# A trunk of one retention and one attention layer: the retention's gates computed 512 columns wide in a place of their own, its transposes and scores moved inside the next unit's projection

## The chip, the cores and the metric

The kernel runs on one core of a Trainium2 chip. A core has five engines that each work through their own list of instructions: TensorE (PE, matrix products; its weight loads are shown as a row of their own, PEld), VectorE (DVE), ScalarE (ACT), GpSimd (POOL) and SyncE (SP, which here only issues the DMA transfers). They meet at semaphores. TensorE writes to PSUM, the accumulator memory of eight banks; the other operands live in SBUF; DRAM is reached by DMA only. The metric is the device time of the whole program in microseconds, the median of three runs.

## The reference, cut to what matters

1024 tokens of width 1024 pass a layer of gated retention and then a layer of gated differential attention. The change touches the retention alone:

```python
proj = h @ w_in_a[layer]                      # h = rmsnorm(x), 1024 x 6144: q, k, v and gate
o = retention(rope(q), rope(k), v)            # 8 heads, q and k 128 wide, v 256 wide, group-normed
y = (o * jax.nn.silu(gate)) @ w_out_a[layer]  # the gate is 2048 wide: 256 columns for each head
x = x + rmsnorm(y, post_norm[layer])
```

The gate of a head depends on the input x alone. It is needed where `o` is multiplied by it, ahead of the output projection.

## The kernel before

**Split products.** All large products are float32 made of three matmuls: both operands are split into a high and a low part (`split`: one ScalarE copy for the high part, one VectorE subtraction for the low part), and `mm3` issues high x high, high x low and low x high for each 128-deep slab (line 100). A product over the model width of 1024 has 8 slabs, so 24 matmuls.

**Units.** The retention runs over 8 heads times 8 chunks of 128 tokens: 64 units, head by head. In a unit, `gemm_qkv` makes q, k and v (512 columns) of one chunk in 24 matmuls. `rotate` applies the rotary tables (two VectorE products, lines 207 and 208, and a GpSimd sum, line 209) and splits v. `gate_and_transpose` makes the 256 gate columns of this head and chunk in another 24 matmuls, then transposes q and k on TensorE (lines 218 and 219), copies them out (line 220) and applies SiLU to the gate (line 221). The unit before this one is finished meanwhile: `score` (line 234, two halves of one fp32 matmul; then lines 235 to 237 for mask and split) sits between slabs 3 and 4 of the next unit's `gemm_qkv`, and `combine` behind that `gemm_qkv`: up to 9 matmuls of 256 columns (tile names `ps<-r,r`), the state's update, the group norm (lines 264 to 268), with the gate multiplied in at line 267, and a store of 128 KB into the DRAM tile `ogd` (line 271).

**What TensorE does in a unit, in order:** 12 matmuls of q/k/v, 2 of the score, 12 of q/k/v, up to 9 of `combine`, 24 of the gate, 2 transposes.

**Weights.** `load_wa` brings a head's weights: eight transfers of 256 KB for q/k/v (12 buffers of tag "w", so four slabs beside the eight in use) and four of 256 KB for the gate (tag "wa", four buffers). Each goes through one of four staging buffers (tag "st") and a `split` (lines 90 and 91). All transfers are issued by SP, in one order.

**What follows.** The output projection goes in two passes over the 8 chunks, heads 0 to 3 and then heads 4 to 7. `prep` loads 512 KB of `ogd` (line 341), transposes it (line 313) and splits it; `gemm0` and `gemm1` make 48 matmuls of 512 columns each; `fin1` transposes the result for the attention layer. Then come the attention's gates (`gate_unit`, tiles `pg<-wbg,x2T`: 24 matmuls of 512 columns for each half of the width and chunk), and its 64 units; neither is touched.

**The order of the instructions** is not the order in the code. A planner in the compiler goes through the instructions by priority (their place in the code), knows each one's cost by a model, and gives every engine a fixed list; a later instruction may go ahead where an earlier one is not ready or has no buffer yet. [...]

Of the kernel before, what the change touches and what calls it, by code (L numbers as in the profile page):

```python
# [18 lines left out]
P = 128  # L19
# [16 lines left out]
def yoco_kernel(ctx: ExitStack, tc: tile.TileContext, a: dict):  # L36
# [11 lines left out]
    gd = dram.tile([S, D], F32, name="gd")  # L48

# [18 lines left out]
    def kt(shape, nm, dt=F32):  # L68
        return sbuf("k", shape, dt, nm)
# [68 lines left out]
    def load_qkv(h, s, tiles):  # L138
        w = wt([P, 2, 512], f"wq{h}{s}")
        tiles.append(w)  # L140
        st = st_([P, 512], "stw")
        nc.sync.dma_start(st, a["wa"][h, s, :, 0:512])
        split(w[:, 0, :], w[:, 1, :], st, g_pre0[:, s : s + 1])

    def load_gate(h, s, tiles):
        if s % 4 == 0:
            w = wta([P, 4, 2, 256], f"wg{h}{s}")
            tiles += [w[:, i] for i in range(4)]
        st = st_([P, 2, 256], "stg")
        nc.sync.dma_start(st, a["wa"][h, s : s + 2, :, 512:768].rearrange("s p c -> p s c"))  # L150
# [3 lines left out]
    def load_wa(h):  # L154
        wq, wg = [], []
        for s in range(NS):
            load_qkv(h, s, wq)
            if s % 2 == 1:
                load_gate(h, s - 1, wg)
        return wq, wg  # L160
# [3 lines left out]
    wq, wg = [], []  # L164
# [16 lines left out]
    w_next = (wq, wg)  # L181
# [10 lines left out]
    def rotate(u):  # L192
        c = u["c"]
        pq, pp, wg = u["pq"], u["pp"], u["wg"]
# [18 lines left out]
    def gate_and_transpose(u):  # L213
        c, qk, qkT = u["c"], u["qk"], u["qkT"]
        pgt = u["pp"][:, 0:256]
        mm3(pgt, [(*xs(c, s), u["wg"][s][:, 0, :], u["wg"][s][:, 1, :]) for s in range(NS)])
        pt = ps("s", 256)
        nc.tensor.transpose(pt[:, 0:P], qk[:, 0:P], ident)
        nc.tensor.transpose(pt[:, P:256], qk[:, P:256], ident)
        nc.scalar.activation(qkT, pt, AF.Copy)  # L220
        nc.scalar.activation(u["og"], pgt, AF.Silu, scale=rstd[:, c : c + 1])
# [19 lines left out]
    def combine(u):  # L241
# [3 lines left out]
        pU, pk = u["pp"][:, 512:768], u["pp"][:, 768:1024]  # L245
# [9 lines left out]
        if c < NC - 1:  # L255
# [15 lines left out]
        nc.sync.dma_start(ogd[c * P : (c + 1) * P, h * DV : (h + 1) * DV], og)  # L271

    prev = None
    early = [ps("g"), ps("g")]
    gemm_qkv(list(enumerate(early)), w_next[0], range(NS))
    for i in range(H * NC):
        h, c = divmod(i, NC)
        if c == 0:
            wq, wg = w_next
        u = {"h": h, "c": c, "wg": wg, "pp": ps("s2", 1024)}  # L280
        u["pq"] = early[i] if i < 2 else ps("g")
        if i >= 2:
            gemm_qkv([(c, u["pq"])], wq, range(0, NS // 2))
        if prev:
            score(prev)
        if i >= 2:
            gemm_qkv([(c, u["pq"])], wq, range(NS // 2, NS))
        rotate(u)
        if prev:
            combine(prev)  # L290
        gate_and_transpose(u)
        prev = u
        if h == 0 and c + 2 < NC:
            if c + 3 < NC:
                load_x(c + 3)
            stats_x(c + 2)
        if c == (1 if h else 5) and h + 1 < H:
            w_next = load_wa(h + 1)
    score(prev)
    combine(prev)  # L300

    def load_wo(src, f, gain, hi, lo):
# [3 lines left out]
        return hi, lo  # L306

# [20 lines left out]
    wo0 = [load_wo(a["woa"], f, None, xw[0][:, f, :], xw[1][:, f, :]) for f in range(4)]  # L328

    def wo_pair():  # L330
        w = wta([P, 2, D], "wo")
        return w[:, 0], w[:, 1]

    wo0 += [load_wo(a["woa"], f, None, *wo_pair()) for f in range(4, 8)]
# [375 lines left out]
def _layout(i):  # L710
# [7 lines left out]
    g = w[:, 4096:6144].reshape(D, H, DV)  # L718
    wa = np.concatenate([qk.reshape(D, H, 256), v, g], axis=2)
    wa = wa.reshape(NS, P, H, 768).transpose(2, 0, 1, 3)  # L720
# [13 lines left out]
        "wa": wa,  # L734
        "woa": np.asarray(i["w_out_a"])[0],
# [25 lines left out]
```

## Time and profile before

| | |
|---|---|
| median of 3 runs (lowest to highest) | 1524.19 us (1524.13 to 1524.55) |
| the profiled execution's own time | 1519.59 us |
| its span, first to last instruction | 1517.8 us |
| PE, PEld busy | 1480.0 us (98%), 1296.0 us (85%) |
| DVE, ACT, POOL busy | 782.9 us (52%), 626.3 us (41%), 266.2 us (18%) |
| DMA moved | 125.63 MB |
| granted TensorE clock over the span | 0.997 |

A row of the groups gives line, engine, operation, output and inputs by the program's names, shape and count, then busy microseconds in all, mean nanoseconds of one, and the idle time of the engine ahead of them. As TensorE overlaps the tail of one matmul with the start of the next, the mean of one is longer than what one costs; the difference of start times in the timeline is the cost. A row of the timeline gives start, duration from the first start to the last end, engine, line, operation and count, and in brackets the idle time ahead of it with what ended it. A row of the stretches gives, for a stretch of time, its length and the busy time and instruction count of PE, PEld, DVE, ACT and POOL, then the granted clock, the share of the DMA engines and the rate.

### The profile page before, as it was taken

What the parts mean: (1) busy time and instruction counts of PE and PEld (TensorE: products, weight loads), DVE (VectorE), ACT (ScalarE), POOL (GpSimd) and SP (SyncE); (2) the same over time, 40 slices, a digit from 0 to 9 for tenths busy, and PEclk for the clock granted to TensorE, in tenths of its full rate; (3) what the DMA queues carried; (4) which work ended last, traced back from release to release, by engine and by line L of the source; (5) the groups of instructions that cost most, each with busy time, mean ns of one, the idle gap of its engine ahead of it and who ended that gap; (6) DMA issues with size and microseconds to landing.
All of it is one profiled execution on the core that took longest, in us unless ns stands there. A gap on an engine that the chain in (4) does not pass through costs nothing.

```text
span 1517.8 us, 23752 instructions
## 1 busy us (share of the span) xinstructions
PE 1480.0 (98%) x8752; PEld 1296.0 (85%) x8752; DVE 782.9 (52%) x1968; ACT 626.3 (41%) x1591; POOL 266.2 (18%) x470
## 2 busy tenths in 40 slices
PE   6999999999999999999999999999999999999998
PEld 5888998888889888888877788988988988987786
DVE  5664645454545443541145511667567577577543
ACT  5542424242424232342244522456455466465421
POOL 1322222212222222200000000222222222222100
PEclk9999999999999999999999999999999999999999
DMA  7430302021211210353244522111011011023352
GB/s 272 146 111 15 97 15 88 22 82 31 60 53 47 62 62 30 98 191 104 98 153 167 190 95 71 34 47 52 10 51 51 11 51 51 12 92 115 116 174 84
DMA packets 70308, 125.63 MB, mean 83 GB/s; under 512 B 7600, under 2 KB 40752, under 8 KB 70192
## 3 DMA queue, kind: packets, MB, share of 16 engines
q1 hardware_dynamic: 70192, 124.11, 25.2%
q8 instruction: 69, 1.13, 0.3%
q14 instruction: 47, 0.39, 0.1%
HBM read 94.72 MB, written 29.36 MB: 82 GB/s over the span
## 4 chain that ended last, share of the span: by engine, by line
PE 80%; DVE 6%; DMA 5%; ACT 4%; issue 4%; POOL 1%; SPq 0%; DVEq 0%; POOLq 0%; ACTq 0%
PE pg L100 54%; PE ps L100 14%; PE ps L526 3%; PE ps L562 3%; PE ps L551 2%; DMA stg<-in_wa 1%; ACT pr L534 1%; DMA stw<-in_wa 1%; PE ps L313 1%; DVE wbh L91 1%; PE ps L234 1%; DMA og<-ogd 1%; PE ps L512 1%; DMA xr<-in_x 1%; DVE m L533 1%
## 5 line engine op out<-in xcount | busy, mean ns | idle before, releaser
L100 PE MATMUL pg<-wq,xT 128*128 128x512 f32 x1536 | 387.6, 402 | 8.8 <-ACT wq L90 7.1
L100 PEld LDWEIGHTS pg<-wq,xT 128*128 128x128 f32 x1536 | 281.5, 190 | 65.0 <-ACT wq L90 7.1
L100 PE MATMUL pg<-wbh,x2T 128*128 128x384 f32 x1536 | 334.6, 353 | 0.0
L100 PEld LDWEIGHTS pg<-wbh,x2T 128*128 128x128 f32 x1536 | 256.4, 189 | 13.0 <-issue 9.3
L106 POOL TENSOR_TENSOR m<-m,mhalf 128x1 f32<-128x1 f32 x152 | 83.3, 548 | 652.8 <-DVE m L105 591.2
L100 PE MATMUL ps<-wg,xT 128*128 128x256 f32 x1536 | 194.8, 283 | 0.0
L100 PEld LDWEIGHTS ps<-wg,xT 128*128 128x128 f32 x1536 | 189.1, 192 | 0.1
L534 ACT ACTIVATE pr<-ps,m 128x256 f32<-128x256 f32 (+7 forms) x128 | 94.0, 737 | 92.1 <-DVE m L533 92.1
L209 POOL TENSOR_TENSOR a<-a 128x256 f32<-128x256 f32 x64 | 48.1, 752 | 340.4 <-DVE a L208 324.9
L533 DVE TENSOR_REDUCE m<-ps 128x1 f32<-128x256 f32 (+7 forms) x128 | 91.1, 753 | 0.0
L100 PE MATMUL pg<-wbg,x2T 128*128 128x512 f32 x384 | 87.9, 390 | 0.8 <-DVE wbg L91 0.8
L90 ACT ACTIVATE r<-pg,tabA 128x256 fp32r<-128x256 f32 x64 | 30.1, 470 | 136.7 <-DVE a L208 136.2
L100 PEld LDWEIGHTS pg<-wbg,x2T 128*128 128x128 f32 x384 | 71.8, 188 | 16.0 <-DVE wbg L91 1.2
L100 PEld LDWEIGHTS ps<-r,r 128*128 128x128 f32 x528 | 72.1, 190 | 8.6 <-ACT r L236 2.6
L235 DVE TENSOR_TENSOR a<-ps,tabA 128x128 f32<-128x128 f32 x64 | 18.5, 289 | 116.5 <-PE ps L234 116.5
L100 PE MATMUL ps<-r,r 128*128 128x256 f32 x528 | 74.8, 283 | 2.4 <-ACT r L236 2.0
L562 PE MATMUL ps<-v,wT 128*128 128x128 f32 x576 | 74.7, 275 | 0.0
L562 PEld LDWEIGHTS ps<-v,wT 128*128 128x128 f32 x576 | 73.2, 191 | 0.7 <-DVE m L105 0.4
L503 POOL TENSOR_TENSOR tabB<-tabB 128x256 f32<-128x256 f32 x64 | 48.5, 758 | 127.9 <-DVE tabB L502 127.6
L207 DVE TENSOR_TENSOR a<-pg,tabA 128x256 f32<-128x256 f32 x64 | 27.0, 423 | 80.6 <-PE pg L100 80.5
L236 ACT ACTIVATE r<-a 128x128 fp32r<-128x128 f32 x64 | 19.8, 309 | 111.6 <-DVE a L235 111.5
L100 PE MATMUL pg<-wo,oh 128*128 128x512 f32 x192 | 59.9, 391 | 0.0
(142 smaller groups left out, 2344.0 us busy)
## 6 DMA issues: line engine op xcount, KB each, us to landing
stw<-in_wa SPq DMA_DIRECT2D x64, 256.0 KB, 3.0
stb<-in_wbh SPq DMA_DIRECT2D x64, 192.0 KB, 2.4
xr<-in_x SPq DMA_DIRECT2D x16, 512.0 KB, 4.2
stg<-in_wa SPq DMA_DIRECT2D x32, 256.0 KB, 3.3
ogd<-a SPq DMA_DIRECT2D x64, 128.0 KB, 1.9
sto<-in_woa SPq DMA_DIRECT2D x16, 512.0 KB, 4.8
og<-ogd SPq DMA_DIRECT2D x16, 512.0 KB, 5.0
y0d<-y SPq DMA_DIRECT2D x8, 512.0 KB, 3.2
```

Of the source, the lines that this page charges most:

```text
L90: nc.scalar.activation(hi, src, AF.Copy, scale=scale)
L100: nc.tensor.matmul(out, l, r, start=(first and i == 0), stop=(last and i == n - 1))
L106: nc.gpsimd.tensor_tensor(out=out, in0=t, in1=mhalf[:, 0:n], op=ALU.pow)
L207: nc.vector.tensor_tensor(out=o4(t1), in0=q4, in1=cb, op=ALU.mult)
L209: nc.gpsimd.tensor_tensor(out=qk, in0=t1, in1=t2, op=ALU.add)
L236: nc.scalar.activation(ss[:, 0, :], sc, AF.Copy)
L503: nc.gpsimd.tensor_tensor(out=r[:, 2], in0=r[:, 0], in1=r[:, 1], op=ALU.add)
L526: nc.tensor.matmul(sc[t][:, c0 : c0 + n], q[rows, ql, qs], k[rows, kl, 0:n], start=(i == 0), stop=(i == 2))
L533: nc.vector.tensor_reduce(out=nm[:, t : t + 1], in_=sc[t][:, :nk], axis=AX.X, op=ALU.max, negate=True)
L534: nc.scalar.activation(pr[t][:, :nk], sc[t][:, :nk], AF.Exp, bias=nm[:, t : t + 1], accum_out=s_[:, t : t + 1])
L551: nc.tensor.transpose(pt[:, k - k0 : k - k0 + P], w[:, k : k + P], ident)
L562: nc.tensor.matmul(po, wT[:, kb * P : (kb + 1) * P], v[:, kb % 4], start=(kb == 0), stop=(kb == b))
```

## The change

The gate leaves the unit. `gate(p, c)` makes the gates of two heads at once, 512 columns in 24 matmuls, applies SiLU (ScalarE, 512 wide) and stores 256 KB into a new DRAM tile `gad`. There are 4 pairs of heads times 8 chunks; pair 0 is made in units 2 to 9, pair p in units 16p to 16p + 7, behind the `combine` that is done in that unit. So 32 units carry a gate (a long unit, 24 more matmuls of 512 columns) and the other 32 none (a short unit). Gate weights of pair 0 are loaded at the start, those of pair p behind units 16p - 5 to 16p - 2, as four transfers of 512 KB. `prep` loads the two 256 KB halves of the gate and multiplies them in on VectorE ahead of its transposes.

The transposes move from the end of their own unit into the next unit's `gemm_qkv`, behind its third slab, and the score moves from behind the fourth to behind the fifth. The first two units are rotated one after the other, and both are transposed and scored inside unit 2. The group norm no longer has the gate in it: the factor `svec` goes into the 128 x 1 column `r`, and one VectorE instruction writes the output from PSUM.

At the start the input statistics of three chunks stand ahead of the gate weights. The square for them is written in place, where a scratch tile was used. The first four of the output projection's weight tiles are loaded ahead of the retention's last units, into the buffers of the gate weights.

```diff
-        junk = kt([P, D], "junk")
-        nc.scalar.activation(junk, xr, AF.Square, accum_out=ssq)
+        nc.scalar.activation(xr, xr, AF.Square, accum_out=ssq)
...
+    def load_gate(p, j):
+        w = wta([P, 2, 2, 512], f"wg{p}{j}")
+        st = st_([P, 2, 512], "stg")
+        nc.sync.dma_start(st, a["wg"][p, 2 * j : 2 * j + 2].rearrange("s p c -> p s c"))
         for i in range(2):
-            split(tiles[s + i][:, 0], tiles[s + i][:, 1], st[:, i], g_pre0[:, s + i : s + i + 1])
+            s = 2 * j + i
+            split(w[:, i, 0], w[:, i, 1], st[:, i], g_pre0[:, s : s + 1])
+            wg[p, s] = w[:, i]
...
     stats_x(0)
-    for s in range(0, NS, 2):
-        load_gate(0, s, wg)
-    nc.sync.dma_start(mask, a["mask"])
     load_x(2)
     stats_x(1)
+    stats_x(2)
+    nc.sync.dma_start(mask, a["mask"])
+    for j in range(4):
+        load_gate(0, j)
+    load_x(3)
...
+    def gate(p, c):
+        pg = ps("s2")
+        mm3(pg, [(*xs(c, s), wg[p, s][:, 0, :], wg[p, s][:, 1, :]) for s in range(NS)])
+        sg = sbuf("v", [P, 512], F32, "sg")
+        nc.scalar.activation(sg, pg, AF.Silu, scale=rstd[:, c : c + 1])
+        nc.sync.dma_start(gad[c * P : (c + 1) * P, p * 512 : (p + 1) * 512], sg)
...
-        pU, pk = u["pp"][:, 512:768], u["pp"][:, 768:1024]
+        pp = ps("s2")
+        pU, pk = pp[:, 0:256], pp[:, 256:512]
...
-        nc.vector.scalar_tensor_tensor(out=og, in0=pU, scalar=mv[:, 0:1], in1=og, op0=ALU.subtract, op1=ALU.mult)
-        nc.vector.tensor_scalar(
-            out=og, in0=og, scalar1=r, scalar2=svec[:, c, h : h + 1], op0=ALU.mult, op1=ALU.mult
-        )
+        nc.vector.tensor_scalar(out=r, in0=r, scalar1=svec[:, c, h : h + 1], scalar2=None, op0=ALU.mult)
+        nc.vector.tensor_scalar(out=og, in0=pU, scalar1=mv[:, 0:1], scalar2=r, op0=ALU.subtract, op1=ALU.mult)
...
+    gates = {(c + 2 if p == 0 else 2 * NC * p + c): (p, c) for p in range(H // 2) for c in range(NC)}
+    late = {2 * NC * p - 5 + j: (p, j) for p in range(1, H // 2) for j in range(4)}
...
+        parts = [f for w in waiting for f in ((transpose_qk, w), (score, w))]
+        at = {2: 0, 4: 1} if len(parts) == 2 else {1: 0, 3: 1, 5: 2, 7: 3}
+        for s in range(NS):
+            gemm_qkv([(c, u["pq"])], wq, [s])
+            if s in at:
+                f, w = parts[at[s]]
+                f(w)
+        for w in waiting[:-1]:
+            combine(w)
+        rotate(u)
+        combine(waiting[-1])
+        waiting = [u]
+        if i in gates:
+            gate(*gates[i])
+        if i in late:
+            load_gate(*late[i])
...
+        if i == H * NC - 4:
+            wo0 = [load_wo(a["woa"], f, None, *wo_pair()) for f in range(4)]
...
         nc.sync.dma_start(og, ogd[t * P : (t + 1) * P, grp * D : (grp + 1) * D])
+        for hf in range(2):
+            g = sbuf("v", [P, 512], F32, "g")
+            cs = slice(hf * 512, hf * 512 + 512)
+            nc.sync.dma_start(g, gad[t * P : (t + 1) * P, grp * D + hf * 512 : grp * D + hf * 512 + 512])
+            nc.vector.tensor_tensor(out=og[:, cs], in0=og[:, cs], in1=g, op=ALU.mult)
```

More of the change, by code (lines that the diff above doesn't have):

```diff
@@ L141, in load_qkv @@
         st = st_([P, 512], "stw")
-        nc.sync.dma_start(st, a["wa"][h, s, :, 0:512])
+        nc.sync.dma_start(st, a["wa"][h, s])
         split(w[:, 0, :], w[:, 1, :], st, g_pre0[:, s : s + 1])
[L145 to L150, printed above, removed]
-        for i in range(2):
-            split(tiles[s + i][:, 0], tiles[s + i][:, 1], st[:, i], g_pre0[:, s + i : s + i + 1])
[L154 to L160, printed above, removed]
+    wg = {}
+    def load_gate(p, j):
+        w = wta([P, 2, 2, 512], f"wg{p}{j}")
+        st = st_([P, 2, 512], "stg")
+        nc.sync.dma_start(st, a["wg"][p, 2 * j : 2 * j + 2].rearrange("s p c -> p s c"))
+        for i in range(2):
+            s = 2 * j + i
+            split(w[:, i, 0], w[:, i, 1], st[:, i], g_pre0[:, s : s + 1])
+            wg[p, s] = w[:, i]
     nc.sync.dma_start(gains, a["gains"])
     load_x(0, parts=2)
-    wq, wg = [], []
+    wq = []
     load_qkv(0, 0, wq)
@@ L211, in rotate, with transpose_qk @@
         split(u["v"][:, 0, :], u["v"][:, 1, :], pq[:, 256:512], avec[:, c, u["h"] : u["h"] + 1])
-    def gate_and_transpose(u):
+    def gate(p, c):
[4 more added lines that the diff above has]
+        nc.sync.dma_start(gad[c * P : (c + 1) * P, p * 512 : (p + 1) * 512], sg)
+    def transpose_qk(u):
         c, qk, qkT = u["c"], u["qk"], u["qkT"]
-        pgt = u["pp"][:, 0:256]
-        mm3(pgt, [(*xs(c, s), u["wg"][s][:, 0, :], u["wg"][s][:, 1, :]) for s in range(NS)])
         pt = ps("s", 256)
+        nc.tensor.transpose(pt[:, P:256], qk[:, P:256], ident)
         nc.tensor.transpose(pt[:, 0:P], qk[:, 0:P], ident)
-        nc.tensor.transpose(pt[:, P:256], qk[:, P:256], ident)
         nc.scalar.activation(qkT, pt, AF.Copy)
-        nc.scalar.activation(u["og"], pgt, AF.Silu, scale=rstd[:, c : c + 1])
         if c < NC - 1:
@@ L306, in load_wo, with wo_pair @@
         return hi, lo
+    def wo_pair():
+        w = wta([P, 2, D], "wo")
+        return w[:, 0], w[:, 1]
+    gates = {(c + 2 if p == 0 else 2 * NC * p + c): (p, c) for p in range(H // 2) for c in range(NC)}
+    late = {2 * NC * p - 5 + j: (p, j) for p in range(1, H // 2) for j in range(4)}
+    early = [ps("g"), ps("g")]
+    gemm_qkv(list(enumerate(early)), wq, range(NS))
+    waiting = []
+    for i in range(2):
+        u = {"h": 0, "c": i, "pq": early[i]}
+        rotate(u)
+        waiting.append(u)
+    for i in range(2, H * NC):
+        h, c = divmod(i, NC)
+        if c == 0:
+            wq, w_next = w_next, []
+        u = {"h": h, "c": c, "pq": ps("g")}
+        parts = [f for w in waiting for f in ((transpose_qk, w), (score, w))]
[7 more added lines that the diff above has]
+            combine(w)
+        rotate(u)
+        combine(waiting[-1])
[4 more added lines that the diff above has]
+            load_gate(*late[i])
+        if h == 0 and c + 1 < NC:
+            if c + 2 < NC:
+                load_x(c + 2)
+            stats_x(c + 1)
+        if c == (1 if h else 5) and h + 1 < H:
+            w_next = []
+            for s in range(NS):
+                load_qkv(h + 1, s, w_next)
+        if i == H * NC - 4:
+            wo0 = [load_wo(a["woa"], f, None, *wo_pair()) for f in range(4)]
+    for f in (transpose_qk, score, combine):
+        f(u)
     def transposed(dst_h, dst_l, src):
@@ L327, in yoco_kernel @@
     xw = [xt([P, 4, D], f"xw{hl}") for hl in range(2)]
[L328 to L334, printed above, removed]
+    wo0 += [load_wo(a["woa"], f, None, xw[0][:, f - 4, :], xw[1][:, f - 4, :]) for f in range(4, 8)]
     wo1 = []
@@ L717, in _layout @@
     v = w[:, 2048:4096].reshape(D, H, DV)
-    g = w[:, 4096:6144].reshape(D, H, DV)
-    wa = np.concatenate([qk.reshape(D, H, 256), v, g], axis=2)
-    wa = wa.reshape(NS, P, H, 768).transpose(2, 0, 1, 3)
+    wa = np.concatenate([qk.reshape(D, H, 256), v], axis=2)
+    wa = wa.reshape(NS, P, H, 512).transpose(2, 0, 1, 3)
+    wg = w[:, 4096:6144].reshape(NS, P, H // 2, 512).transpose(2, 0, 1, 3)
     wi = np.asarray(i["w_in_b"])[0]
```

34 lines of the change are left out of this document (4 added, 30 removed).

## The prediction

> **What bounds the kernel now.** I read the page first, then the groups, then a table of stretches, then the timeline of one quiet unit.
>
> ```profile
> span 1517.8 us, 23752 instructions
> ...
> PE 1480.0 (98%) x8752; PEld 1296.0 (85%) x8752; DVE 782.9 (52%) x1968; ACT 626.3 (41%) x1591; POOL 266.2 (18%) x470
> ...
> L100 PE MATMUL ps<-wg,xT 128*128 128x256 f32 x1536 | 194.8, 283 | 0.0
> ...
> L100 PE MATMUL pg<-wbg,x2T 128*128 128x512 f32 x384 | 87.9, 390 | 0.8 <-DVE wbg L91 0.8
> ```
>
> ```profile
> 30.00:45.00 15.00, 12.48 (x67) 10.54 (x68) 10.71 (x28) 11.23 (x23) 7.40 (x11) 0.89 0.61 217
> ...
> 110.00:650.00 540.00, 539.46 (x3313) 483.70 (x3311) 269.89 (x742) 180.76 (x459) 117.24 (x206) 1.00 0.17 54
> ...
> 177.00:187.00 10.00, 10.00 (x62) 8.91 (x61) 8.07 (x20) 5.12 (x14) 2.52 (x5) 1.00 0.55 172
> ...
> 280.00:289.90 9.90, 9.90 (x62) 8.90 (x61) 4.09 (x12) 2.46 (x7) 2.22 (x4) 1.00 0.05 15
> ```
>
> From 110 to 650 us TensorE is busy for 539.46 of 540 us: there the retention is bound by how many matmuls it issues and how long each holds the engine; only what shortens this list can gain. The other engines matter as soon as they make TensorE wait. DMA is at 0.17 there, so extra traffic is cheap. One quiet unit on TensorE:
>
> ```profile
> 300.89 3.04 PE L100 MATMUL ps<-wg,xT 128*128 128x256 f32 x24
> 303.77 0.27 PE L218 MATMUL ps<-ident,a 128*128 128x128 f32 x1
> ...
> 303.91 2.98 PE L100 MATMUL pg<-wq,xT 128*128 128x512 f32 x12
> 306.73 0.38 PE L234 MATMUL ps<-a 128*128 128x128 f32 x2
> 306.86 3.02 PE L100 MATMUL pg<-wq,xT 128*128 128x512 f32 x12
> 309.72 1.24 PE L100 MATMUL ps<-r,r 128*128 128x256 f32 x9
> 310.79 3.04 PE L100 MATMUL ps<-wg,xT 128*128 128x256 f32 x24
> ```
>
> By starts: the gate takes 303.77 - 300.89 = 2.88 us (120 ns a matmul), the two transposes 0.14, the q/k/v halves 2.82 and 2.86 with 0.13 of score between, `combine` 1.07; 9.90 us in all.
>
> **The change part by part.** The sum is made against the profiled execution (span 1517.8, own time 1519.59 us; the 1.8 us around the span stay) and then taken off the median of 1524.19, which lies 4.6 us above it.
>
> *1. The gate at 512 columns.* Removed: 1536 matmuls of 256 columns, 64 x 2.88 = 184.3 us. Added: 768 of 512 columns. The nearest row is the attention's own gate, `pg<-wbg,x2T`: same shape, 24 in a row, and 87.9 / 384 = 229 ns each, so 24 take 5.49 us and 32 gates 175.8 us: **-8.6 us**. Bounds: the q/k/v halves of the unit above, 2.82 + 2.86 = 5.68 us for 24, would give 32 x 5.68 = 181.8 us, -2.6; the fastest stream of 512 columns in the trace, in the output projection,
>
> ```profile
> 666.24 0.61 PE L100 MATMUL pg<-xw,oh 128*128 128x512 f32 x2
> 666.70 0.39 PE L100 MATMUL pg<-xw,ol 128*128 128x512 f32 x1
> 666.92 0.61 PE L100 MATMUL pg<-xw,oh 128*128 128x512 f32 x2
> ```
>
> has three matmuls in 0.68 us, 5.44 us for 24, and would give -10.2. I take the attention's gate because it has the same operands' layout and length; the q/k/v halves each start behind a break, which the new gate does not.
>
> The Trainium skill (TensorE: Matmul & The Clock Gate, Back-to-back issue gap) gives N / 2.4 + 2.5 ns for a lone warm matmul; by that two narrow ones cost only 2.5 ns more than one wide one, and the estimate from that page would be 768 x 2.5 = 1.9 us instead of 8.6. The rows above disagree: twice 120 against 229 is 11 ns.
>
> *2. Transposes, score and `combine`* stay the same in number. A score inside a 512-column stream costs what it cost; a transpose pair now has wide matmuls on both sides as the score has. Zero, if their inputs are there in time. The start-to-start distances on the other engines:
>
> ```profile
> 280.22 0.42 DVE L207 TENSOR_TENSOR a<-pg,tabA 128x256 f32<-128x256 f32 x1 [1.81 <-PE pg L100]
> ...
> 281.12 0.74 POOL L209 TENSOR_TENSOR a<-a 128x256 f32<-128x256 f32 x1 [5.26 <-DVE a L208]
> ...
> 283.97 0.27 PE L218 MATMUL ps<-ident,a 128*128 128x128 f32 x1
> ...
> 284.47 0.32 SPq L271 DMA_DIRECT2D ogd<-a  x1
> 284.54 0.38 ACT L220 ACTIVATE a<-ps 128x256 f32<-128x256 f32 x1
> ...
> 286.93 0.38 PE L234 MATMUL ps<-a 128*128 128x128 f32 x2
> ...
> 288.01 0.29 DVE L237 TENSOR_TENSOR r<-a,r 128x128 fp32r<-128x128 f32 x1 [0.38 <-ACT r L236]
> ```
>
> A short unit takes TensorE 9.90 - 2.88 = 7.02 us. The rotation needs 281.86 - 280.22 = 1.64 us, plus about 0.2 from the end of q/k/v; in the new order 1.07 (`combine`) + 3/4 of 2.82 = 3.2 us lie between, so 1.3 us are spare. From the transposes to copied q and k is 284.92 - 283.97 = 0.95 us, and that had SiLU in front; the new order gives two slabs, 1.4 us, plus the transposes themselves: 0.5 to 0.7 spare. From the score to the split mask is 288.30 - 286.93 = 1.37 us against three slabs, 2.1: 0.7 spare. In a quiet short unit nothing waits; DVE's 4.09 us and ACT's 2.46 fit into 7.02. The output's store is at 284.47, 4.25 us behind the rotation's start, so its buffer is free before the rotation two units later.
>
> The spare times go where weights are split in a short unit:
>
> ```profile
> 246.21 2.68 ACT L90 ACTIVATE wq<-stw,gains 128x512 fp32r<-128x512 f32 x4
> ...
> 246.95 2.08 DVE L91 SCALAR_TENSOR_TENSOR wq<-stw,gains,wq 128x512 fp32r<-128x512 f32 x3 [1.48 <-ACT wq L90]
> ```
>
> One split of 512 columns holds ACT for 0.67 and DVE for 0.69 us. The next head's slabs come in two groups of four, at the last unit of a head and the first of the next (177 to 187 us above is such a place: DVE 8.07 of 10 us). At each of six boundaries one of these two units is short: 24 splits. The gates of pairs 1 to 3 are 12 transfers of two splits: 24 more, all in short units. In a short unit with four splits DVE has 4.09 + 4 x 0.69 = 6.9 of 7.02 us: full, while it was 7 to 8 of 9.9 before. Queued behind a split on DVE or ACT stand lines 207, 220 and 235 to 237, and TensorE waits for those. A split costs 0 if it falls into an idle time and 0.69 at most; spare times of 0.5 to 1.3 us swallow one, not two. I take 0.05 us for each of 48: **+2.5**, range 0 to +6.
>
> *3. The start.* Rows of TensorE:
>
> ```profile
> 22.17 5.91 PE L100 MATMUL ps<-wg,xT 128*128 128x256 f32 x48
> 30.46 0.33 PE L218 MATMUL ps<-ident,a 128*128 128x128 f32 x1 [2.38 <-POOL a L209]
> ...
> 32.13 2.04 PE L100 MATMUL pg<-wq,xT 128*128 128x512 f32 x4 [1.23 <-DVE r L91]
> ...
> 38.46 0.33 PE L218 MATMUL ps<-ident,a 128*128 128x128 f32 x1 [0.82 <-POOL a L209]
> ...
> 52.26 1.10 PE L100 MATMUL ps<-r,r 128*128 128x256 f32 x7 [0.40 <-DVE r L237]
> ...
> 63.37 1.62 PE L100 MATMUL ps<-r,r 128*128 128x256 f32 x9 [1.14 <-ACT r L236]
> ```
>
> Idle: 2.38 + 1.23 + 0.82 + 0.40 + 1.14 = 6.0 us, and the granted clock of 0.89 over 30 to 45 us costs 15 x 0.11 = 1.65 more: 7.6 us that a better order could recover. The new order asks for chunk 2 of x ahead of the gate weights and goes straight on to unit 2, with two rotations for cover. Against that stand twice the gate weights at once (four times 512 KB, eight splits of 0.69 on DVE, where lines 207 to 237 of two units, three statistics and two splits of x stand in the same queue). I take half: **-4**, range -7.6 to 0. Squaring in place moves no work.
>
> *4. Storing and reloading the gate.* 32 stores of 256 KB at a DMA share of 0.17 cost nothing; SP waits for SiLU ahead of each, and behind it stand only loads with units to spare. The reload meets a busier place:
>
> ```profile
> 796.95 1.06 PE L313 MATMUL ps<-ident,og 128*128 128x128 f32 x8 [1.63 <-DMA og<-ogd]
> ...
> 825.52 1.06 PE L313 MATMUL ps<-ident,og 128*128 128x128 f32 x8 [1.39 <-DMA og<-ogd]
> ```
>
> ```profile
> 779.28 0.69 DVE L369 TENSOR_TENSOR y<-pg,y 128x512 f32<-128x512 f32 x1 [0.46 <-PE pg L100]
> ```
>
> ```profile
> gd<-vg SPq DMA_DIRECT2D x16, 256.0 KB, 2.0
> ```
>
> Two preparations of the second pass already wait for `ogd`. There the first multiplication, like line 369 about 0.69 us, comes on top, and 256 KB of gate (2.0 us) beside each `ogd` load may delay it. In the first pass both lie behind a whole `gemm0`. I take 0.7 for the product and 0.3 for traffic at each of the two: **+2**; range 0 (the gate is there early and other waits absorb it) to 2 x (2.0 + 0.7) = +5.4.
>
> *5. The end of the retention.*
>
> ```profile
> 648.44 0.27 PE L218 MATMUL ps<-ident,a 128*128 128x128 f32 x1
> ...
> 649.44 0.49 PE L234 MATMUL ps<-a 128*128 128x128 f32 x2 [0.18 <-ACT a L220]
> 650.78 0.50 PE L100 MATMUL ps<-r,r 128*128 128x256 f32 x2 [0.85 <-ACT r L236]
> ```
>
> The last unit's rotation was covered by its gate (2.88 us); now `combine` (1.07) and the first transposes of the output projection must cover it. Its weights come earlier. The idle 0.18 + 0.85 here becomes about 1.7: **+0.7**, range -1 to +2.
>
> Sum: -8.6 + 2.5 - 4 + 2 + 0.7 = **-7.4 us**, so 1524.19 - 7.4 = **1516.8 us**.
>
> **The rivals.**
>
> *A. Width is worth little*: in this stage a wide matmul holds TensorE as long as in the q/k/v halves, 5.68 us for a gate. For it: those rows are of this very stage; against it: they are broken streams. Then -2.6 in place of -8.6: 1522.8. The page's rule above, worked from rows, is nearly this case.
>
> *B. The order is better than I credit*: the start recovers its 7.6, splits and reload cost 0.5 each, the end nothing: -8.6 - 7.6 + 1.0 = -15.2, 1509.0.
>
> *C. Slower: the splits in short units.* DVE is full there (6.9 of 7.02), and its list was laid out by a model; if each of the 48 splits costs half its length, 0.35 us, term 2 is 16.8 instead of 2.5 and the sum +6.9: 1531.1. The change turns slower from (8.6 + 4 - 2 - 0.7) / 48 = 0.21 us a split. For it: two splits in a row exceed the spare times; against it: 177 to 187 us shows DVE at 81% and TensorE at 10.00 of 10.
>
> *D. The reload binds the second pass*: its preparations come in four pairs, and if each pair waits 2.0 + 0.7 us, term 4 is 10.8: sum +1.4, 1525.6. Against it: only two waits for `ogd` before.
>
> That the planner undoes the weaving is possible, but TensorE's list then has the same matmuls: term 1 stands, and it is no case of its own.
>
> **How the numbers follow.** Forecast 0.65, A 0.08, B 0.10, C 0.11, D 0.06. The likeliest is 1516.8, with its own range of 1511 to 1522. About 0.2%, 3 us, can be told from no change. Faster: 0.60 of the forecast, B's 0.10, 0.02 of A: 0.72. Same: 0.05 of the forecast, 0.06 of A, 0.05 of D: 0.16. Slower: C and 0.01 of D: 0.12. The range of 1508 to 1527 leaves out most of C and the better half of B.
>
> **What would show it.** Term 1: 768 matmuls `ps<-wg,xT` of 512 columns, 24 of them 5.4 to 5.6 us apart from first start to next group (5.7 for A). Term 2: waits of `ps<-ident,a`, `ps<-a` and `ps<-r,r` in units 10 to 15, 24 to 31, 40 to 47 and 56 to 63 that add up to 2 or 3 us (over 10 for C). Term 3: TensorE idle and clock between 22 and 65 us. Term 4: waits of the transposes at line 313's place for VectorE's product rather than for a DMA. The forecast is wrong if TensorE's busy time falls by less than 5 us, or if its idle time outside the start grows by more than 8.

## The result and the profile after

| | before | after |
|---|---|---|
| median (lowest to highest) | 1524.16 us (1522.31 to 1524.55) | 1534.82 us (1533.54 to 1535.96) |
| the profiled execution's own time | 1519.59 us | 1535.96 us |
| its span | 1517.8 us | 1534.2 us |
| granted TensorE clock | 0.997 | 0.989 |

The ratio is 1.0075, with a 95% interval of 1.0062 to 1.0088: the change costs about 11 us, where 7.4 us of gain were forecast. The page of the kernel after, its span, engines, and the two wide streams of the retention:

```profile
span 1534.2 us, 22154 instructions
...
PE 1486.0 (97%) x7984; PEld 1260.2 (82%) x7984; DVE 796.4 (52%) x1968; ACT 619.3 (40%) x1527; POOL 279.7 (18%) x470
...
L101 PE MATMUL ps<-wg,xT 128*128 128x512 f32 x768 | 180.9, 390 | 0.0
```

There are 768 matmuls fewer, as meant, and yet TensorE is busy 6.0 us longer. That looks like a contradiction until the time is cut at four marks: TensorE's first matmul, the score of unit 15, the score of unit 63, the first matmul of the attention's gate, the last matmul. The table of stretches of the kernel before between these marks (length; busy time and count of PE, PEld, DVE, ACT, POOL; granted clock; DMA share; GB/s):

```profile
7.08:179.39 172.31, 165.64 (x969) 145.17 (x970) 101.32 (x272) 80.70 (x181) 39.63 (x67) 0.99 0.38 122
179.39:649.44 470.05, 469.58 (x2885) 421.13 (x2883) 235.93 (x648) 157.27 (x400) 102.08 (x179) 1.00 0.18 57
649.44:854.46 205.02, 198.68 (x957) 163.19 (x957) 74.34 (x110) 69.86 (x112) 9.52 (x16) 1.00 0.43 147
854.46:1510.50 656.04, 645.71 (x3947) 566.46 (x3945) 367.37 (x931) 314.49 (x894) 113.74 (x201) 1.00 0.22 70
```

The same four of the kernel after:

```profile
6.92:181.92 175.00, 165.77 (x779) 135.76 (x780) 96.50 (x250) 76.45 (x157) 40.85 (x65) 0.98 0.40 132
181.92:650.44 468.52, 465.17 (x2302) 386.80 (x2301) 240.74 (x643) 156.28 (x363) 113.80 (x180) 1.00 0.24 80
650.44:867.99 217.55, 206.27 (x960) 169.11 (x961) 87.38 (x136) 67.76 (x110) 9.80 (x17) 0.96 0.48 156
867.99:1526.80 658.81, 648.39 (x3946) 568.57 (x3945) 367.75 (x931) 314.85 (x894) 113.98 (x201) 0.99 0.22 70
```

Length minus busy is idle time. The clock column hides the rest: the records of the clock show nothing but 1.0 and 0.5, and a stretch at 0.5 costs up to half of the time for which TensorE is busy in it (its idle time there is already counted as idle). Summed from those records, the half-clock stretches are 3.41 us long before, with TensorE busy for 2.9 (1.4 us lost), and 30.7 us after, with TensorE busy for 27.4 (13.7 us lost). Taken apart, after minus before, in us:

| stage | work at full clock | idle | lost to the clock | sum |
|---|---|---|---|---|
| start, to the score of unit 15 | -1.7 | +2.6 | +1.9 | +2.7 |
| retention, to the score of unit 63 | -4.4 | +2.9 | 0 | -1.5 |
| end of retention and output projection | +0.2 | +4.9 | +7.4 | +12.5 |
| attention | -0.4 | +0.1 | +3.1 | +2.8 |
| **all** | **-6.3** | **+10.5** | **+12.3** | **+16.5** |

The first matmuls, ahead of the first record (which begins 14.5 us into the span before and 12.8 us after), also come at half speed, 15 of them in 7.0 busy us before and 12 in 5.6 us after; the 0.7 us that this costs less after stand in the start's work.

The work fell by some 6 us, less than the 8.6 that the wide gate was to save. Idle time took that back, and the clock added more still. The attention's 3.1 us lie in code that was not touched: in 11 of the 14 traces of this document the clock falls at that place, and the profile before is one of the three in which it does not.

The profile before was a quick execution, so 16.5 us stand here against 10.7 between the medians. The medians show the same cause. The four runs of the kernel after have a granted clock of 0.989 to 0.990; 60 further runs of the kernel before, taken beside the experiments, have 0.991 to 0.997, and 0.995 in the middle. The difference of 0.006, over some 1525 us, is about 9 us (an estimate, and an upper one, since idle time at half clock is in it).

**Where the work became less.** A quiet long unit and a quiet short unit on TensorE after the change:

```profile
378.74 5.63 PE L101 MATMUL ps<-wg,xT 128*128 128x512 f32 x24
384.20 2.21 PE L101 MATMUL pg<-wq,xT 128*128 128x512 f32 x9
...
387.86 0.38 PE L236 MATMUL ps<-a 128*128 128x128 f32 x2
...
400.35 0.38 PE L236 MATMUL ps<-a 128*128 128x128 f32 x2
```

```profile
302.28 0.38 PE L236 MATMUL ps<-a 128*128 128x128 f32 x2
...
309.33 0.38 PE L236 MATMUL ps<-a 128*128 128x128 f32 x2
```

The gate takes 384.20 - 378.74 = 5.46 us; a long unit 12.49, a short one 7.05, together 19.54 for two units that took 2 x 9.90 = 19.80.

**Where idle time came.** The end of the retention, TensorE after (to be held against the prediction's rows from 648.44 us on):

```profile
647.83 0.52 PE L101 MATMUL ps<-r,r 128*128 128x256 f32 x3
649.47 0.33 PE L221 MATMUL ps<-ident,a 128*128 128x128 f32 x1 [1.12 <-POOL a L207]
...
650.44 0.49 PE L236 MATMUL ps<-a 128*128 128x128 f32 x2 [0.53 <-ACT a L223]
651.73 1.65 PE L101 MATMUL ps<-r,r 128*128 128x256 f32 x6 [0.80 <-ACT r L238]
654.35 1.11 PE L334 MATMUL ps<-ident,og 128*128 128x128 f32 x4 [0.97 <-DVE a L271]
656.15 0.79 PE L101 MATMUL pg<-wo,oh 128*128 128x512 f32 x1 [0.69 <-ACT oh L88]
```

Each step of the last unit's chain now waits for the step ahead of it: rotation, copy, mask, group norm, split; 4.1 us of waits where the kernel before had 0.18 + 0.85. Before, the unit's own gate covered the rotation, and the first matmuls of the output projection lay between the later steps (the row at 651.27 in the next fence); after, the first of them starts at 656.15. The kernel before, right behind the last row that the prediction shows of it there:

```profile
651.27 0.96 PE L100 MATMUL pg<-xw,oh 128*128 128x512 f32 x3
```

**And where the clock fell.** The same place after the change, in stretches of about 3.4 us:

```profile
644.20:647.60 3.40, 3.40 (x20) 2.87 (x19) 1.53 (x6) 0.46 (x2) 0.84 (x2) 1.00 0.55 178
647.60:651.00 3.40, 1.68 (x11) 1.04 (x9) 2.24 (x6) 1.44 (x4) 1.38 (x2) 1.00 0.29 75
651.00:654.40 3.40, 1.70 (x7) 1.41 (x7) 2.79 (x10) 0.35 (x2) 1.39 (x2) 0.51 0.19 54
654.40:657.90 3.50, 2.81 (x10) 2.17 (x11) 1.67 (x4) 0.66 (x2) 0.55 (x1) 0.50 0.50 146
657.90:661.30 3.40, 3.40 (x14) 2.78 (x12) 1.39 (x2) 1.13 (x2) 0.00 (x0) 0.50 0.75 240
661.30:664.70 3.40, 3.40 (x17) 2.81 (x16) 1.92 (x2) 1.57 (x2) 0.00 (x0) 1.00 0.46 158
```

A stretch in which TensorE was busy 1.68 of 3.40 us (49%) is followed by one at half clock; that one, busy 50%, and the next, busy 80%, leave the clock where it is; only after a full one does it come back. TensorE was busy for 7.9 of these 10.24 us, so they cost up to 4.0 us, as much again as the 4.1 us of waits.

**The second pass of the output projection.** What TensorE waits for there, before and then after (us in all, times, longest):

```profile
PE ps L313 <- DMA og<-ogd: 3.0, 2, 1.6
PE ps L313 <- DVE x2T L88: 2.0, 3, 0.8
```

```profile
PE ps L334 <- DVE x2T L89: 4.8, 3, 2.2
PE ps L334 <- DVE og L361: 3.1, 2, 1.7
PE ps L334 <- DVE ol L89: 0.6, 2, 0.3
```

5.0 us became 8.5. The preparations wait for VectorE's product (line 361) where they had waited for the DMA, and the transposes behind them for VectorE's splits (line 89), which stand in its list around those products. Two of these waits also fell into stretches that turned the clock down, for 3.4 us together.

### The profile page after: what moved, and what is told of

Read it like the earlier page. It is cut to its first block, busy times and chain, and to the rows that moved or that the text cites. A ratio compares the mean times of both kernels' runs of the same rounds, so it can differ in the third digit from the quotient of the medians.

```text
span 1534.2 us, 22154 instructions
## 1 busy us (share of the span) xinstructions
PE 1486.0 (97%) x7984; PEld 1260.2 (82%) x7984; DVE 796.4 (52%) x1968; ACT 619.3 (40%) x1527; POOL 279.7 (18%) x470
## 4 chain that ended last, share of the span: by engine, by line
PE 79%; DVE 7%; DMA 4%; ACT 4%; issue 4%; POOL 1%; SPq 0%; DVEq 0%; POOLq 0%; ACTq 0%
PE pg L101 52%; PE ps L101 14%; PE ps L546 3%; PE ps L582 3%; PE ps L571 2%; ACT pr L554 1%; PE ps L334 1%; DMA og<-ogd 1%; DVE wbh L92 1%; PE ps L236 1%; PE ps L532 1%; POOL m L107 1%; DMA stw<-in_wa 1%; DMA stx<-in_xT 1%; DVE m L553 1%
## 5 line engine op out<-in xcount | busy, mean ns | idle before, releaser
L101 PE MATMUL pg<-wq,xT 128*128 128x512 f32 x1536 | 398.6, 403 | 8.3 <-ACT wq L91 6.9
L107 POOL TENSOR_TENSOR m<-m,mhalf 128x1 f32<-128x1 f32 x152 | 90.2, 593 | 673.3 <-DVE m L106 611.7
L101 PE MATMUL ps<-wg,xT 128*128 128x512 f32 x768 | 180.9, 390 | 0.0
L101 PEld LDWEIGHTS ps<-wg,xT 128*128 128x128 f32 x768 | 141.7, 188 | 27.8
L207 POOL TENSOR_TENSOR a<-a 128x256 f32<-128x256 f32 x64 | 52.9, 826 | 203.8 <-DVE a L206 180.3
L101 PE MATMUL ps<-r,r 128*128 128x256 f32 x528 | 78.3, 287 | 6.0 <-ACT r L238 3.4
L91 ACT ACTIVATE r<-pg,tabA 128x256 fp32r<-128x256 f32 x64 | 30.3, 473 | 114.8 <-DVE a L206 109.4
L215 ACT ACTIVATE sg<-ps,rstd 128x512 f32<-128x512 f32 x32 | 22.1, 690 | 118.1 <-PE ps L101 118.1
L231 POOL TENSOR_TENSOR r<-a,r 128x128 fp32r<-128x128 f32 x56 | 30.5, 545 | 187.8 <-ACT r L230 184.9
```

Of the source, the lines that this page charges most:

```text
L91: nc.scalar.activation(hi, src, AF.Copy, scale=scale)
L101: nc.tensor.matmul(out, l, r, start=(first and i == 0), stop=(last and i == n - 1))
L107: nc.gpsimd.tensor_tensor(out=out, in0=t, in1=mhalf[:, 0:n], op=ALU.pow)
L207: nc.gpsimd.tensor_tensor(out=qk, in0=t1, in1=t2, op=ALU.add)
L215: nc.scalar.activation(sg, pg, AF.Silu, scale=rstd[:, c : c + 1])
L231: nc.gpsimd.tensor_tensor(out=qq[:, 1, :], in0=qkT[:, 0:P], in1=f32(qq[:, 0, :]), op=ALU.subtract)
```

## The experiments

Runs of one kernel differ by some microseconds (the kernel before: 1519.9 to 1531.2 us over all of them), so each ratio is against runs of the kernel before on the same chip.

### What the parts at the two ends cost

*No gate at the preparations.* Load and product left out, so the output is not gated.

```diff
-        for hf in range(2):
-            g = sbuf("v", [P, 512], F32, "g")
...
-            nc.vector.tensor_tensor(out=og[:, cs], in0=og[:, cs], in1=g, op=ALU.mult)
```

> The changed kernel without the reload of the gate in the output projection: neither the 32 loads of 256 KB nor the 32 products on VectorE; the output is therefore that of ungated retention. Theory 1 (what was lost lies in short idle times of TensorE at the end of the retention, in the second pass and at the start, and in the stretches at half clock that follow each): the second pass gets back about 3.5 us of idle time and up to 3.4 us of clock, the end of the retention keeps its half clock; time 1527 to 1531. Theory 2 (the reload is the loss, by its traffic and its products): all of the 12.5 us between the last score and the first attention gate comes back; time 1520 to 1523. Theory 3 (the short units of the retention are the loss): no change, 1533 to 1536.

Measured: 1526.82 us (1523.05 to 1531.92), ratio 1.0013 [0.9997, 1.0030]. So loading and multiplying at the preparations is worth 8 of the 11 us, far more than the 2 us forecast for it; about 5 of the 8 are clock, by the granted clock of all runs (0.9925 in the middle of these ten, 0.989 in the kernel after; an estimate). What is left is no gain, though the wide gate saves its work here too.

*One half each.* The loads without the product, and a product without the loads (the tile with itself); neither applies the gate.

> The changed kernel with the gate's 32 loads of 256 KB kept and the product with it left out (the output is that of ungated retention). Without both, the time was 1526.8. If the traffic and its place in SP's order are what the reload costs: 1532 to 1536, as with the product. If it is the product, which stands in VectorE's list ahead of other work and between the load and the transposes: 1526 to 1528.

> The changed kernel without the gate's 32 loads, but with a product of the same size on VectorE in its place: each half of the loaded tile is multiplied by itself (the output is not the reference's). If the traffic is the cost: 1526 to 1528, as without both. If the product is: 1532 to 1536.

Measured: loads alone 1539.56 us, ratio 1.0085 [1.0059, 1.0110]; product alone 1529.47 us, 1.0039 [1.0026, 1.0053]. The first doesn't price the traffic: with no product to wait for, the planner moved loads ahead into the retention's last units (30 of the 32 were issued before 636 us, 7 in the kernel after), where TensorE then waited 9.4 us for copies on ScalarE, which itself waited there for transfers. The two halves don't add up to the whole, as each changes the planner's order.

What the product does is seen in the second pass, from its first to its last matmul, less what the clock cost there: 105.9 us before, 106.5 with the weaving alone (below), 107.1 with the loads alone, 109.4 with the product alone, 109.8 in the kernel after, and 109.7 to 110.3 in six other kernels of this document that have the whole product. So VectorE's product in the chain is enough to lengthen the second pass by about 4 us, without the traffic. One profile does not fit: with neither load nor product it took 109.8 us too, because the transposes waited 7.2 us for two loads of `ogd`. That profile is the slowest of its ten runs, so it can't show where the 8 us came back.

*A gate for the last unit.* The gate of unit 55 (pair 3, chunk 7) moved to unit 63, and the output projection's first weights loaded into the buffers of x instead.

```diff
+    gates[H * NC - 1] = gates.pop(H * NC - 1 - NC)
```

> The changed kernel with one gate moved: that of pair 3 and chunk 7 is made in unit 63 instead of 55, so that the last rotation has 24 matmuls of 512 columns over it; the first four output weight tiles go into the buffers of x, the other four into those of the gate weights, as these stay in use longer. Theory 1: idle time around the last unit falls from 4.1 us to 1.5 or less and the 10.24 us at half clock that begin at 651 us are gone, worth 2.6 + 5.1 us; time 1526 to 1528. Theory 2: no change there, 1533 to 1536. Theory 3: no change.

Measured: 1532.91 us (1532.05 to 1535.19), ratio 1.0059 [1.0044, 1.0074]. The wait of 1.12 us for the rotation was gone, but the chain behind it still waited (0.83, 0.85, 0.82, 0.39 and 0.69 us), and the clock fell to half at the same place, for 6.83 us. One cover for the first step of a chain is not enough.

*Needless matmuls at the end.* 17 matmuls of 512 columns into an unused bank, between the steps of the last unit. Nobody reads their results.

```diff
-    for f in (transpose_qk, score, combine):
+    for n, f in ((5, transpose_qk), (3, score), (4, combine)):
+        warm(n)
         f(u)
+    warm(5)
```

> The changed kernel with 17 needless matmuls of 512 columns, whose results nobody reads, put into TensorE's list where it stood idle around the last unit: 5 ahead of the last transposes, 3 ahead of the score, 6 and 1 in the last combine, 2 ahead of the output projection's first transposes. They are 17 x 0.227 = 3.9 us of work in 4.1 us of idle time. Theory 1 (a stretch of 3.4 us in which TensorE is busy for less than about half is followed by half clock until a stretch is nearly full): the 10.24 us at half clock after 651 us are gone, or down to one stretch, although the waits themselves stay; from the last score to the first attention gate 5 us less, time 1529 to 1531. Rival (the half clock is not set off by the idle time, or costs nothing as the engines wait for each other there): no change, 1534 to 1536, or 1 to 3 us more for the added work.

Measured: 1531.19 us (1528.82 to 1534.43), ratio 1.0049 [1.0032, 1.0067]. More work, and about 3.6 us less time, though the intervals of the two ratios still touch. The end of the retention with the filler (line 330):

```profile
644.96 1.32 PE L330 MATMUL pg<-xT 128*128 128x512 f32 x5
...
647.78 0.49 PE L236 MATMUL ps<-a 128*128 128x128 f32 x2 [0.57 <-ACT a L223]
...
652.57 0.73 PE L101 MATMUL pg<-wo,oh 128*128 128x512 f32 x2 [0.69 <-ACT oh L88]
```

The first matmul of the output projection comes 652.57 - 647.78 = 4.8 us behind the last score instead of 5.7, and the half clock here is gone. From the last score to the attention's first gate it is 213.1 us instead of 217.6. Over its eight runs the granted clock is 0.990 to 0.994, against 0.989 to 0.990 in the kernel after. The work done in the gaps was worthless, so what it won is the clock: this speaks for the idle time as what sets it off.

### What the order costs

*The weaving alone.* The kernel before with transposes and score moved into the next unit, and the narrow gate kept in each unit.

```diff
-        gate_and_transpose(u)
+        gate(u)
...
+        at = {2: 0, 4: 1} if len(parts) == 2 else {1: 0, 3: 1, 5: 2, 7: 3}
```

> The kernel before with the weaving alone: transposes behind the third and score behind the fifth slab of the next unit's projection, the first two units rotated and gated one after the other, gates still 256 columns wide in each unit, multiplied in where they were. No short units, no reload, and the last unit keeps its gate. Theory 1: no place where TensorE runs dry is new, so the time is that of before within 3 us, 1521 to 1527. Theory 2: the same. Theory 3 (in its form that the woven order itself makes TensorE wait): 1530 or more.

Measured: 1528.36 us (1525.72 to 1531.98), ratio 1.0028 [1.0015, 1.0040]. A quiet unit, from gate to gate:

```profile
301.82 3.04 PE L100 MATMUL ps<-wg,xT 128*128 128x256 f32 x24
...
311.76 0.52 PE L100 MATMUL ps<-wg,xT 128*128 128x256 f32 x3
```

9.94 us instead of 9.90, and the units at the heads' boundaries take 10.4 to 10.6 instead of 9.9. The weaving gains nothing by itself and costs some 4 us; it is only needed because half of the units have lost the gate that covered their rotation.

*The score one slab earlier.*

```diff
-        at = {2: 0, 4: 1} if len(parts) == 2 else {1: 0, 3: 1, 5: 2, 7: 3}
+        at = {1: 0, 3: 1} if len(parts) == 2 else {1: 0, 3: 1, 5: 2, 7: 3}
```

> The changed kernel with transposes behind the second and the score behind the fourth slab, in place of third and fifth: 12 matmuls instead of 9 between a score and its combine, 6 instead of 9 between combine and transposes. Theory 3 (the first unit of the six head boundaries loses 0.4 to 0.75 us as the weights' splits stand ahead of the mask's split on VectorE, with only 2.1 us between score and combine): from score 15 to score 63 the 4.6 us that are lost against the sum of the quiet units fall to 1 or 2; time 1531 to 1533. If the loss moves to the transposes, which now have 0.7 us less: no change or slower, 1534 to 1538.

Measured: 1531.28 us (1530.73 to 1534.38), ratio 1.0048 [1.0030, 1.0065]. One kind of boundary was mended (12.5 us for unit 23 instead of 12.9); at the other, unit 15 took 7.2 us instead of 7.8 and the one behind it 13.1 instead of 12.5. Score 15 to score 63 gained nothing (469.2 us, 468.5 in the kernel after).

*All gates eight units later*, so that the last eight units have one and the start has none.

```diff
-    gates = {(c + 2 if p == 0 else 2 * NC * p + c): (p, c) for p in range(H // 2) for c in range(NC)}
+    gates = {2 * NC * p + NC + c: (p, c) for p in range(H // 2) for c in range(NC)}
```

> The changed kernel with every gate moved eight units later, so that the pair's gates are made in its odd head (units 8 to 15, 24 to 31, 40 to 47, 56 to 63) and the first pair's weights are loaded behind units 3 to 6 instead of at the start; the output weight tiles as in last_gate_63. Theory 1: the end is covered as in last_gate_63 (-8 us), and the start no longer has eight splits and 2 MB in front of it: of its 8.4 us of idle time and 3.4 us of clock a half comes back; time 1519 to 1523. Theory 2: the second pass is as before the move, 1533 or a little less for the start. Theory 3: the number of short units is the same, so no change but for the start, 1529 to 1533.

Measured: 1531.18 us (1528.13 to 1534.53), ratio 1.0049 [1.0034, 1.0065]. The start was 3.3 us shorter in the profiled execution, but the output projection's stage was nearly as long as in the kernel after (214.7 us; 217.5). So it is not the lack of a gate in the last eight units alone that makes this stage long.

### The wide gate without the weaving

A gate need not be made in one go: its PSUM bank can stay open over two units. So each unit issues 12 matmuls of 512 columns where the kernel before had 24 of 256, and transposes, score and `combine` stand where they stood before. So do the loads at the start and the buffers of the output projection's weights, so more than the weaving is undone here.

```diff
+    def half_gate(i):
+        k, part = divmod(i, 2)
+        p, c = divmod(k, NC)
+        if part == 0:
+            gt["pp"] = ps("s2", 1024)
+        r = range(part * 4, part * 4 + 4)
+        mm3(gt["pp"][:, 0:512], [(*xs(c, s), wg[p, s][:, 0, :], wg[p, s][:, 1, :]) for s in r], part == 0, part == 1)
```

In a first version `combine` used the other half of the same two-bank PSUM tile. In a second one the odd heads' gate was also reloaded in their own unit and multiplied in the group norm, as before, which leaves half of the product to the preparations.

> The wide gate kept, the weaving undone: every unit issues 12 matmuls of a 512-column gate (half of one gate, whose PSUM bank stays open over two units) in the place where the kernel before had its 24 narrow ones, and transposes, score and combine stand where they stood before. Store, reload and the product at the preparations stay as in the changed kernel, and so do the gate weights per pair of heads. Theory 1 (the width is worth what a quiet unit shows, and the changed kernel loses it to its order: short units, uncovered end, clock): a quiet unit takes 7.02 + 2.73 = 9.75 us against 9.90, score of unit 15 to score of unit 63 about 466 us against 475, the end as before, the second pass 3 to 4 us slower by the product; 1518 to 1522 us, faster than before by 0.1 to 0.4%. Theory 2 (the width itself gains little once other engines share the time): 1524 to 1530 us.

> As half_gates, but the odd heads' gate (128 KB for each unit) is reloaded in their unit and multiplied in the group norm, as before; only the even heads' half is multiplied at the preparations (two products of 256 columns in place of two of 512). Theory 1 (the product ahead of the transposes costs the second pass 3 to 4 us): half of that comes back, second pass 107 to 108 us, total 1 to 2 us below half_gates. Theory 2 (traffic or place of the loads costs it, not the length of the product): no gain, within 1 us of half_gates.

Measured: 1587.26 us, ratio 1.0422 [1.0399, 1.0445], and 1567.31 us, 1.0290 [1.0266, 1.0315]: the worst of all. What TensorE waits for from 110 to 650 us in the first of them:

```profile
PE ps L219 <- POOL a L205: 15.3, 50, 1.0
PE ps L101 <- DVE a L269: 9.5, 42, 0.5
```

Line 269 is the last read of `combine`'s half of the shared tile: the gate's matmuls, which write the other half, are ordered behind it. The planner answers by putting them elsewhere, ahead of the rotation instead of over it, and the transposes wait for it (line 205). The width was not what cost; the shared tile was. So `combine` got a bank of its own:

```diff
-        pp = u["pp"]
+        pp = ps("s")
         pU, pk = pp[:, 0:256], pp[:, 256:512]
```

> As half_gates, with the state and output of combine in a PSUM bank of their own (tag s) instead of sharing the tile of the open gate; nothing else changed. TensorE's list then has in each unit what the kernel before has, in its order, with 12 matmuls of 512 columns for 24 of 256. Theory 1 (half_gates lost its time to the shared tile: each half gate waited for the group norm's last read; the width itself is worth what a quiet unit shows): a quiet unit takes 9.75 us (9.90 before), score of unit 15 to score of unit 63 about 466 us (470 before), end as before, second pass 3 to 4 us slower by the product, half the clock's losses gone; 1517 to 1522 us. Theory 2 (half gates in this place are slow by themselves): a quiet unit over 10 us, 1530 us or more.

> As half_gates2, but the odd heads' gate (128 KB for each unit) is reloaded in their unit and multiplied in the group norm, as before; only the even heads' half is multiplied at the preparations (two products of 256 columns in place of two of 512). Theory 1 (the product ahead of the transposes costs the second pass 3 to 4 us): half of that comes back, second pass 107 to 108 us, total 1 to 2 us below half_gates2. Theory 2 (traffic or place of the loads costs it, not the length of the product): no gain, within 1 us of half_gates2.

Measured: half gates 1523.35 us (1521.12 to 1526.65), ratio 1.0000 [0.9991, 1.0010]; with the odd heads' gate multiplied in their unit **1518.71 us (1515.10 to 1519.89), ratio 0.9966 [0.9953, 0.9979]**. This last version is faster than both kernels. Its quiet unit, from score to score:

```profile
308.10 0.38 PE L234 MATMUL ps<-a 128*128 128x128 f32 x2
...
317.90 0.38 PE L234 MATMUL ps<-a 128*128 128x128 f32 x2
```

And its first three stretches between the same marks:

```profile
6.83:171.58 164.75, 162.04 (x777) 132.98 (x777) 99.10 (x262) 76.93 (x159) 40.48 (x66) 1.00 0.46 147
171.58:639.24 467.66, 465.15 (x2306) 387.82 (x2304) 237.98 (x657) 152.57 (x359) 106.55 (x181) 1.00 0.23 76
639.24:850.16 210.92, 202.12 (x960) 166.15 (x961) 85.87 (x144) 69.73 (x112) 9.51 (x16) 0.98 0.50 163
```

A unit takes 9.80 us instead of 9.90. The start is 7.6 us shorter than in the kernel before: its idle time is 2.7 us instead of 6.7 and the clock never falls there; which part of the order does that wasn't tried. The output projection still costs 5.9 us more than before (3.1 of it the clock), so the reload remains the price of the width here. The granted clock of its runs, 0.994 in the middle, is no higher than that of the kernel before (0.995), so its gain is not one of the clock. Halving the product was worth 4.6 us between the two medians, more than the 1 to 2 expected; the second pass itself explains about 2.6 of that (109.4 against 112.0 us, with one half-clock stretch in each). Another 3.1 us between the profiles is clock in the attention, which is not touched; over all runs the granted clock is 0.994 against 0.992, about 3 us by estimate.

## Why the prediction was wrong, step by step

**1. The gate at 512 columns: right.** 5.46 us a gate against 5.49 taken. In two quiet units 0.26 us are saved, 8.3 over the 64, against 8.6 forecast; rival A is out. The formula of the Trainium skill (TensorE: Matmul & The Clock Gate, Back-to-back issue gap), with 1.9, is out too.

**2. Transposes, score and splits in short units: the size was in the range, the place only in part.** From the score of unit 15 to that of unit 63, 24 quiet pairs would have gained 6.2 us; 1.5 were gained, so 4.7 were lost, with 2.5 taken and up to 6 allowed. Nothing like rival C's 0.35 us for each split happened: most short units with splits take 7.05 us like the others. That C's time, 1531.1 us, comes nearest to the measured one is chance. The loss sits in a few places, above all the units before a boundary (15, 31 and 47 take 7.77 us, 23 and 39 take 12.9 and 13.0) and units 60 to 62 (7.79, 7.31 and 7.95), where the output projection's weights are split. The latter was said in step 5 ("its weights come earlier") and priced at nothing. The weaving, priced at zero where inputs are in time, costs 0.04 us in every unit as well.

**3. The start: failed.** -4 was taken, and the stage came out at +2.7, with the width's own -2.1 in it: for the order alone +4.8 instead of -4. Waits of TensorE in the start after the change:

```profile
22.76 0.33 PE L221 MATMUL ps<-ident,a 128*128 128x128 f32 x1 [1.43 <-POOL a L207]
...
33.62 0.50 PE L101 MATMUL ps<-r,r 128*128 128x256 f32 x2 [1.86 <-ACT r L238]
35.13 0.50 PE L101 MATMUL ps<-r,r 128*128 128x256 f32 x2 [1.01 <-DVE r L239]
...
50.56 0.79 PE L236 MATMUL ps<-a 128*128 128x128 f32 x2 [2.39 <-ACT a L223]
```

The step counted the waits that the new order removes and took half of them. It named what stands against it, twice the gate weights and two units' small steps in the queues of ACT and VectorE, but gave that no price. These are the waits above: the first for the rotation's sum on GpSimd, the others for copies and masks on ACT and VectorE. Copies of this start in the other experiments took 170.7 to 176.1 us, so some of it is chance, but none came near the forecast's 166 (172.3 - 2.1 of width - 4). That a start can be had for 164.8 us the half gates show.

**4. Storing and reloading: the mechanism right, the size too small.** The product is late at two preparations, as said. What was left out: it shares VectorE with the splits of the transposes next to it, which are late in their turn (4.8 us instead of 2.0). Waits of +3.5 us and two stretches of half clock stand against +2. Rival D has the place right; its price of 2.7 at each of four pairs is too high for the waits alone.

**5. The end of the retention: failed.** Rotation cover was the only thing counted, for +0.7. The rest of the chain lost its cover too, since nothing of the output projection came between, and 4.1 us of waits stand where 1.0 were, with up to 4.0 us of half clock on top.

**The step that is missing.** The largest item, 12.3 of the 16.5 us between the profiles, is in no term: what idle time does to the clock of the work behind it. Step 3 priced one such stretch in the start as something to be won back. It should have been a price on every new wait: steps 3, 4 and 5 each added waits of 1 to 2 us in a row, and half clock followed in each of these stages.

The Trainium skill (TensorE: Matmul & The Clock Gate, Part 1) describes this gate: half rate after at least one idle window of about 3.4 us, full rate after a busy one, with a window that runs free. This case's trace agrees on the two rates and on the length (stretches of 3.41 us), but not on "idle": 1.68 of 3.40 us busy was enough to lose the clock, and 2.81 of 3.50 not enough to regain it.

The forecast named two conditions under which it would be wrong. TensorE's busy time did not fall; it rose, through half-clock matmuls that are longer. And idle time outside the start grew by 7.9 us, just under the 8 named.

## What to carry to other kernels

Where TensorE is nearly always busy (539.5 of 540 us here), a saving of work is easily smaller than what its new order costs; first look for a way to make the saving in the old order (here by leaving a PSUM bank open over two units), and give tiles that are written by different chains a PSUM tile each. Price a wait not only by its length: several waits that leave TensorE busy for half or less of some 3.4 us can cost up to 1.7 us more in each 3.41-us stretch behind them, until one is nearly full. When work that covered a chain is moved away, walk the whole chain, in the last unit above all, and ask of each step what covers it now.

## What the runs showed of the hardware

**The clock reacts to half-busy stretches.** More of them in the kernel after, at other places (length, then the busy time of TensorE and the other engines; the clock is the third column from the end):

```profile
46.90:50.30 3.40, 1.27 (x6) 0.71 (x4) 1.23 (x1) 3.10 (x4) 0.00 (x0) 1.00 0.71 257
...
801.20:804.60 3.40, 1.80 (x8) 1.14 (x7) 0.68 (x2) 0.00 (x0) 0.00 (x0) 1.00 0.92 305
808.10:811.50 3.40, 1.25 (x8) 0.85 (x9) 2.62 (x5) 1.18 (x2) 0.00 (x0) 1.00 0.83 277
...
1415.60:1419.10 3.50, 1.50 (x14) 1.00 (x10) 2.44 (x6) 0.59 (x2) 1.63 (x3) 0.99 0.65 197
1419.10:1422.50 3.40, 2.71 (x10) 2.16 (x10) 2.11 (x3) 2.17 (x5) 0.00 (x0) 0.50 0.00 0
```

Shares of 37% to 43% turned the clock down, 53% here did not; 80% did not bring it back. The half-clock stretches lie on a fixed raster of 3.41 us, so whether a given wait fills half of one is chance. With this raster laid through all 14 traces, half clock followed each of the 45 full-clock stretches in which TensorE was busy for less than 45%, 14 of the 52 between 45% and 60%, and none above 60%. At half clock, all 24 stretches with 82% or less kept it, and all 59 with 83% or more ended it.

Chance of this kind would account for a good part of the spread between runs of one kernel. The 60 runs of the kernel before agree: the longer a run, the lower its granted clock (correlation -0.71), and 0.006 between the highest and lowest clock is some 9 of the 11.3 us of spread. No experiment moved the raster, so this stays read off and not shown.

**A GpSimd instruction is slow beside a VectorE instruction with two SBUF operands.** After, near the end of the retention, first GpSimd and then VectorE:

```profile
643.15 1.46 POOL L107 TENSOR_TENSOR m<-m,mhalf 128x1 f32<-128x1 f32 x1 [0.48 <-DVE m L106]
```

```profile
643.00 1.21 DVE L89 TENSOR_TENSOR wol<-sto,woh 128x1024 fp32r<-128x1024 f32 x1
```

The same instruction takes 0.55 us where VectorE leaves it alone; here it waits out a VectorE instruction with two SBUF operands, and the group norm with it. All 152 of them take 0.55 us in the kernel before; after, eleven take 0.99 to 1.46 us, and beside each of these stands such a VectorE instruction. Another 58 start beside a VectorE instruction that reads one operand from PSUM, and still take 0.55. The Trainium skill (SBUF — State Buffer, SBUF: two separate sides) says that these two engines lock a port pair against each other for a whole instruction when VectorE has two SBUF inputs; the rows agree.
